# Layer 0 of a two-layer encoder: earlier gate modulation, conformer taps at other places, the short conv's taps beside the output projection

## The chip, the cores and the metric

The kernel runs as one program on one core of a Trainium2 chip. The metric is the device time of one execution in microseconds (us), lower is better. A core has a matrix engine (TensorE, PE), a vector engine (VectorE, DVE), a scalar engine (ScalarE, ACT), GpSimd (POOL), and SyncE (SP), whose queue issues the DMA transfers here. Each engine takes its instructions in the order of its own queue; an instruction that waits holds up all that stand behind it on that queue.

## The reference

For each of two layers, on x of 256 positions by 2048 channels, with a condition vector c:

```python
mod = (silu(c) @ w_mod[l] + b_mod[l]).reshape(bn, 6, d)
shift_m, scale_m, gate_m, shift_f, scale_f, gate_f = ...
h = layer_norm(x) * (1.0 + scale_m) + shift_m
uv, q_c, kv_c, k_r, sb, sc, sh, ag = split(h @ w_in[l])
y_a = gmlp_mixer(uv, ...)                 # u * (W_s LN(v) + b), 128-position blocks
y_b = mla_mixer(q_c, kv_c, k_r, ...)      # attention from latents, rotary key
y_c = sb * causal_dwconv(sc * sh, w_conv) # short conv, 3 taps
y_d = conformer_conv(ag, ...)             # GLU, 31 taps, LayerNorm, swish
y = concatenate([y_a, y_b, y_c, y_d]) @ w_out[l]
x = layer_norm(ALPHA * x + (1.0 + gate_m) * y, ...)
h = layer_norm(x) * (1.0 + scale_f) + shift_f
x = layer_norm(ALPHA * x + (1.0 + gate_f) * conv_ffn(h, ...), ...)
```

Everything is float32. Many products are made of three products of split numbers (a high part "hi" and a remainder "lo", both in the faster fp32r form): lo is made on DVE by a subtraction (L462, tile wlo), hi on ACT by a cast (L461, tile whi).

## The kernel before, in words

**Stages of layer 0.** The shared normalised input is made in five pieces over the contraction; within each, products of the conformer's (D), gMLP's (U, V) and short conv's gate (E) columns are accumulated (`by_pieces`, PIECES). Then come, in the order of TensorE's work:

- the latents, stage **B** (`latent_group`, eight units of two contraction tiles, tiles B_w and B_n, exact fp32 products). Beside them DVE does the gMLP's norm (`mix_v`, tile va, L1004 to L1032) and TensorE its mixing products (ps_mix). At its end `mix_b` squares and copies the latents on ACT (L1062 to L1075);
- the short conv's columns, stage **C** (`group`, eight units, tile C_c). The attention (`attend`, which starts with the transposes ps_q at L1087) is "postponed": its instructions come behind the first unit of C. At the end `mix_c` multiplies into chC, `conv_c` makes three taps over four channel blocks (one ACT scaling and two DVE multiply-adds a block, L1250 to L1261, tile yc), and `mix_e` multiplies by the gate E (L1264);
- the **output projection** (`out_proj`, tile o). Its first chunk of 1024 columns has eight units of two contraction tiles, and the order of the contraction is a, b, c, d: yc is read from its ninth tile on. Two more chunks of 512 columns follow with exact products ("plain": 1024 and 1536).

**What runs beside them.** `stream` is called once for each unit: it issues the unit's weight load, then the products of the unit before, then pumps the modulation, then takes some blocks from a list called `background`:

```python
item = load()
flush()
pending.append(lambda: products(item))
if mods:
    pump()
for _ in range(min(bg, len(background))):
    background.pop(0)()
```

The **modulation stream** (`mod_stream`) loads w_mod in rows of 128x2048 (1024 KB, tile wmod, SP's queue) and adds each into an accumulator with one DVE multiply-add (L240, tile macc; the first of a sum is L238). Sixteen loads make one vector; GATE_M comes first in layer 0, then SHIFT_F and SCALE_F; all 48 are needed by the end of the output projection. For a gate, a bias row is loaded behind the sixteenth (L354, tile brow) and added on DVE (L358); then `gate_rows` lets TensorE sum it over the partitions (ps_gate, four quarters, as "chores" of later pumps). For a shift or scale the sum is ps_mod. `pump` adds the stage's rate in RATES to a credit and takes one step for each whole credit. The loads' buffers are four "raw" tiles; split weights and bias rows use the same four, so a modulation load on SP's queue waits until DVE has used the load four back, and weights queued behind it on SP wait as well.

The **background** of layer 0 is the conformer's 31 taps and its norm (`conv_d` with `taps`: four ACT scalings to the tile scaled, L919, in two buffers, then one DVE addition to convD, L920; norm_d at the end). STEPS says how many are taken per unit: one in B, three in C. What is left at the end of C is drained there.

The queue of each engine is laid out when the program is built, by a scheduler that follows these calls and its own costs; a product can thus stand ahead of, or behind, others that the source names in another order.

Of the kernel before, what the change touches and what calls it, by code (L numbers as in the profile page):

```python
# [18 lines left out]
KT = D // P  # L19
# [13 lines left out]


RATES = [
    dict(B=1.6, C=2.2, out=1.5, up=0.7, down=0.7),
    dict(D=1.0, U=0.0, V=0.0, B=0.0, C=0.0, E=0.9, out=0.6, up=0.3, down=0.7),
]

STEPS = [  # L40
    dict(B=1, C=3, up=2),
    dict(U=7, B=4, C=4, E=8, up=2),
]

PIECES = ((0, 2), (2, 2), (4, 4), (8, 4), (12, 4))
# [5 lines left out]
def encoder_kernel(ctx: ExitStack, tc: tile.TileContext, A: dict, consts: bass.AP, out: bass.AP):  # L51
# [321 lines left out]
    def phase(l, name):  # L373
        pace["rate"] = RATES[l][name]
# [26 lines left out]
    def drain_background():  # L401
        while background:
            background.pop(0)()
# [214 lines left out]
    def run(g):  # L618
        units, load, products, end, bg = g
        for u in range(units):  # L620
            stream(lambda: load(u), lambda item, u=u: products(item, u), bg)
            pending.extend(postponed)
            postponed.clear()
        pending.append(end)
# [44 lines left out]
    def out_proj(l, w, src, order, gate_of, name, post_g, post_b, before, then, plain=(), bg=0):  # L669
# [113 lines left out]
        for c0, width in CHUNKS:  # L783
            last = c0 + width == D
            nk = 2048 // width
            units = nkt // nk
            state = {"tail": []}

            def load(u, c0=c0, width=width, nk=nk, units=units, last=last):
                item = load_unit(u, c0, width, nk, units, last)  # L790
                if last and u == units - 1:
                    gains()
                return item

            def load_unit(u, c0, width, nk, units, last):
                kt = order[nk * u]
                assert order[nk * u : nk * u + nk] == list(range(kt, kt + nk))
                spare = nk if last and units - 4 <= u < units - 2 else 0
                exact = c0 in plain
                parts = weights(w, kt, nk, c0, width, exact, spare)  # L800
                s4 = src[kt // 4]
                if exact:
                    return parts, [(s4[:, kt % 4 + k, :], None) for k in range(nk)]
                acts = []
                for k in range(0, nk, 2):
                    pair = kept.get(kt + k)
                    if pair is None:
                        pair = act_pair("a")
                        split(pair, s4[:, kt % 4 + k : kt % 4 + k + 2, :])
                        if nkt == KT:  # L810
                            kept[kt + k] = pair
                    for j in range(2):
                        acts.append([h[:, j, :] for h in pair[:2]])
                return parts, acts

            def unit(item, u, state=state, c0=c0, width=width, nk=nk, last=last, units=units):
                if u == 0:
                    state["ps"] = [
                        [acc_tile(f"{name}_{c0}{t}{i}") for i in range(width // 512)] for t in range(2)
                    ]  # L820
                if last and u >= units - 4:
                    state["tail"].append((item, u))
                    return
                for t in range(2):
                    products(t, item, state["ps"], u, nk)

            for u in range(units):
                stream(lambda: load(u), lambda item, u=u, unit=unit: unit(item, u), bg, not last)

            def done(state=state, c0=c0, nk=nk, last=last):  # L830
                if c0 == 0:
                    box["gate"] = gate_of()
                for t in range(2):
                    for item, u in state["tail"]:
                        products(t, item, state["ps"], u, nk)
                    if t == 0 and last and before is not None:
                        before()
                for t in range(2):
                    finish(t, state["ps"], c0)
                    if last:  # L840
                        norm(t)
                if last:
                    closed.append(True)

            pending.append(done)


    def mixers(l, w_in, Y, hF=None, between=None):
# [397 lines left out]

        def conv_c(ch):
            yc = Y["c"] = slot("yc").rearrange("p (j s) -> p j s", j=4)
            for j in range(4):
                act.activation(out=yc[:, j, :], in_=ch[:, j, :], func=AF.Copy, scale=SW(2, j))  # L1250
                for k in range(2):
                    dve.scalar_tensor_tensor(
                        out=yc[:, j, 2 - k :],
                        in0=ch[:, j, : S - 2 + k],
                        scalar=SW(k, j),
                        in1=yc[:, j, 2 - k :],
                        op0=ALU.mult,
                        op1=ALU.add,
                    )

        def mix_e(cps, _):  # L1261
            yc = Y["c"]
# [36 lines left out]
    def by_pieces(l, w_in, hF, between, mix_d, mix_u, gelu_v, mix_v, mix_b, mix_c, mix_e):  # L1299
# [49 lines left out]
        for q, (k0, nkt) in enumerate(PIECES):  # L1349
            ahead = between(q + 1) if q + 1 < len(PIECES) else ([], None)  # L1350
            exact = k0 < PLAIN_KT
            loaded = {}

            def load(g, kt):

                c0, width = (C_AG, 1024) if g == "D" else (cols[g], 512)
                nk = min(2048 // width, nkt)
                for j, p in enumerate(weights(w_in, kt, nk, c0, width, exact or g != "D")):
                    loaded[(g, kt + j)] = p

            mods_left = list(ahead[0])
            units = len(mods_left)

            def some_mods(share):
                while mods_left and (units - len(mods_left)) < units * share:
                    mods_left.pop(0)()

            def d_part(kt, half):
                if ("D", kt) not in loaded:
                    load("D", kt)  # L1370
                chan_major(accD, kt, loaded[("D", kt)], range(4 * half, 4 * half + 4), kt == 0, kt == KT - 1)

            turns_d = [(kt, h) for kt in range(k0, k0 + nkt) for h in range(2)]
            n = len(turns_d) // 4
            for s in range(4):
                mine = turns_d[s * n : (s + 1) * n]
                if ("D", mine[0][0]) not in loaded:
                    load("D", mine[0][0])
                some_mods((0.3, 0.7, 1.0, 1.0)[s])
                if s == 3 and ahead[1] is not None:  # L1380
                    ahead[1]()
                for kt, h in mine:
                    d_part(kt, h)
                if s < 3:
                    g = "UVE"[s]
                    load(g, k0)
                    some_mods((0.5, 0.85, 1.0)[s])
                    side(g, [(kt, loaded[(g, kt)]) for kt in range(k0, k0 + nkt)], k0, nkt)
        mix_d(accD, None)
        mix_u(sums["U"], None)  # L1390
        for t in range(2):
# [5 lines left out]

        def mix_ce(cps, tps):
            mix_c(cps, tps)
            mix_e(sums["E"], None)  # L1400

        run(group(w_in, C_SC, 1024, f"C{l}", mix_ce, hF=hf, bg=STEPS[l]["C"]))
        drain_background()
# [151 lines left out]
    for l in range(DEPTH):  # L1555
        Y = {}
        if l == 0:
            hF = [slot(f"hF{q}").rearrange("p (j s) -> p j s", j=4) for q in range(4)]
            mixers(l, A["w_in"][l], Y, hF, lambda q: piece(q, hF))
        else:  # L1560
            mixers(l, A["w_in"][l], Y)
        phase(l, "out")
        flush()
        out_proj(
            l,
            A["w_out"][l],
            [Y[n] for n in "abcd"],
            list(range(KT)),
            gate(l, GATE_M),
            f"o{l}",  # L1570
            A["post_mix_g"][l],
            A["post_mix_b"][l],
            needs(l, SHIFT_F, SCALE_F),
            modulated(l, SHIFT_F, SCALE_F),
            plain=(1024, 1536) if l == 0 else (),
        )
        phase(l, "up")
        if l + 1 < DEPTH:
            turns.extend(load_params(l + 1))
        G = []  # L1580
        ffn_up(l, G)
        phase(l, "down")
        flush()
        out_proj(
            l,
            A["ffn_w_down"][l],
            G,
            list(range(NF)),
            gate(l, GATE_F),
            f"d{l}",  # L1590
            A["post_ffn_g"][l],
            A["post_ffn_b"][l],
            needs(l + 1, SHIFT_M, SCALE_M) if l + 1 < DEPTH else None,
            modulated(l + 1, SHIFT_M, SCALE_M) if l + 1 < DEPTH else None,
        )
# [63 lines left out]
```

## Time and profile before

| | us |
|---|---|
| median of 3 runs (2279.96 to 2282.76) | 2281.75 |
| the profiled execution | 2284.06 |
| its span in the trace | 2282.3 |
| TensorE busy | 2216.6 (97%) |
| VectorE busy | 1781.2 (78%) |
| ScalarE busy | 1111.3 (49%) |
| stage B of layer 0 | 189.92 to 233.89 |
| stage C with attention | 233.89 to 330.46 |
| first chunk of the output projection | 330.46 to 388.47 |
| the other two chunks | 388.47 to 448.75 |

A profile is one execution; the time outside the span is 1.76 us. Rows of its views read so: a timeline row is start, duration, engine, line of the kernel, operation, tile written <- tiles read, shapes, and how many records the row joins; in brackets is the engine's idle time in front of it and what ended that. A group row is the same without a start: count, then total busy time, mean of one in ns, then the idle time ahead of these instructions. "PEclk" is the TensorE clock that was granted, as a share of full speed. An fp32 matmul leaves two records.

### The profile page before, as it was taken

To read this page: it belongs to the slowest core of one execution; us is meant where nothing else is said; L and a number is where in the kernel's file an instruction comes from. 1 tells how busy PE (TensorE), PEld (TensorE's weight loads), DVE (VectorE), ACT (ScalarE), POOL (GpSimd) and SP (SyncE) were. 2 spreads that over 40 slices of the span, in tenths; PEclk is the share of its full clock that TensorE was granted. 3 is DMA by queue.
4 is the path that set the end of the run, shared out by engine and by line. 5 is a ranking of instruction groups with operands and counts; after the bars stand their busy time and mean duration, and the time that the engine had idled before them with its cause. 6 is when DMAs were issued, how large, how long until landed. Compare 5 with 4: busy or idle time off the path is not lost. (4 is left out here: it accounts for less than half of the span.)

```text
span 2282.3 us, 28994 instructions
## 1 busy us (share of the span) xinstructions
PE 2216.6 (97%) x11118; PEld 1823.0 (80%) x11118; DVE 1781.2 (78%) x2192; ACT 1111.3 (49%) x1693; POOL 37.2 (2%) x61
## 2 busy tenths in 40 slices
PE   5899999999999999999999999999999999999997
PEld 4686777478888888887886888877888888888886
DVE  6877889588899899898977997887776565565676
ACT  2234652264554554544556545556555454454553
POOL 2000000000000000000000000000000000000000
PEclk9999999999999999999999999999999999999999
DMA  9999879778888988888875755966665555555554
GB/s 348 368 336 337 334 261 379 282 263 327 309 326 300 333 312 327 318 318 295 323 269 195 236 186 175 328 247 226 240 224 183 195 182 194 190 196 187 197 190 147
DMA packets 228691, 604.11 MB, mean 265 GB/s; under 512 B 14580, under 2 KB 27108, under 8 KB 206788
## 3 DMA queue, kind: packets, MB, share of 16 engines
q1 hardware_dynamic: 227704, 601.25, 74.3%
q8 instruction: 87, 1.43, 0.2%
q0 software_dynamic: 848, 1.01, 0.1%
q14 instruction: 52, 0.43, 0.0%
HBM read 600.11 MB, written 2.10 MB: 264 GB/s over the span
## 5 line engine op out<-in xcount | busy, mean ns | idle before, releaser
L461 ACT CAST whi<-wraw 128x1024 fp32r<-128x1024 f32 (+1 forms) x624 | 649.7, 1048 | 705.6 <-PE g_c L79 198.6
L462 DVE TENSOR_TENSOR wlo<-wraw,whi 128x1024 fp32r<-128x1024 f32 (+1 forms) x624 | 749.0, 1214 | 309.0 <-ACT whi L461 301.8
L79 PE MATMUL v_c<-hT,whi 128*128 128x512 f32 x1408 | 491.4, 393 | 0.0
L79 PE MATMUL g_c<-hT,whi 128*128 128x512 f32 x1280 | 446.8, 393 | 0.0
L79 PE MATMUL v_c<-hT,wlo 128*128 128x256 f32 x1408 | 394.1, 280 | 0.0
L79 PE MATMUL d<-whi,a 128*128 128x512 f32 x1344 | 387.9, 390 | 0.0
L240 DVE SCALAR_TENSOR_TENSOR macc<-wmod,cact,macc 128x2048 f32<-128x2048 f32 x150 | 352.0, 2347 | 18.2 <-DMA wmod<-in_w_mod_dram 18.0
L79 PE MATMUL g_c<-hT,wlo 128*128 128x256 f32 x1280 | 358.2, 280 | 0.0
L79 PEld LDWEIGHTS v_c<-hT,whi 128*128 128x128 f32 x1408 | 263.6, 187 | 59.5
L79 PEld LDWEIGHTS d<-whi,a 128*128 128x128 f32 x1344 | 252.8, 188 | 52.6
L79 PEld LDWEIGHTS g_c<-hT,whi 128*128 128x128 f32 x1280 | 239.7, 187 | 54.3
L79 PEld LDWEIGHTS v_c<-hT,wlo 128*128 128x128 f32 x1408 | 265.8, 189 | 0.2
L79 PEld LDWEIGHTS g_c<-hT,wlo 128*128 128x128 f32 x1280 | 241.7, 189 | 0.2
L79 PE MATMUL d<-wlo,a 128*128 128x512 f32 x672 | 233.7, 390 | 1.9 <-DVE wlo L462 1.9
L79 PEld LDWEIGHTS d<-wlo,a 128*128 128x128 f32 x672 | 126.5, 188 | 29.0 <-DVE wlo L462 2.7
L79 PE MATMUL o<-whi,a 128*128 128x512 f32 x352 | 102.4, 398 | 0.0
L480 ACT CAST a<-g 128x512 fp32r<-128x512 f32 x132 | 81.3, 617 | 36.0 <-PE d L79 33.3
L481 DVE TENSOR_TENSOR a<-g,a 128x512 fp32r<-128x512 f32 x132 | 87.8, 685 | 1.8 <-ACT a L480 1.8
L605 PE MATMUL first<-wexact,hN 128*128 128x512 f32 x192 | 85.5, 595 | 1.2 <-ACT hN L82 0.8
L240 DVE SCALAR_TENSOR_TENSOR qacc<-wmod,cact,qacc 128x1024 f32<-128x1024 f32 (+1 forms) x75 | 80.2, 1070 | 2.4 <-DMA wmod<-in_w_mod_dram 0.4
L79 PEld LDWEIGHTS o<-whi,a 128*128 128x128 f32 x352 | 67.1, 192 | 15.3 <-ACT whi L461 1.0
L1448 DVE SCALAR_TENSOR_TENSOR u<-g,pf,u 128x254 f32<-128x254 f32 (+1 forms) x176 | 73.8, 479 | 0.4 <-ACT u L82 0.2
(355 smaller groups left out, 2497.6 us busy)
## 6 DMA issues: line engine op xcount, KB each, us to landing
wraw<-in_ffn_w_up_dram SPq DMA_DIRECT2D x168, 1024.0 KB, 5.2
wmod<-in_w_mod_dram SPq DMA_DIRECT2D x160, 1024.0 KB, 6.5
wraw<-in_ffn_w_down_dram SPq DMA_DIRECT2D x88, 1024.0 KB, 5.2
wmod<-in_w_mod_dram SPq DMA_DIRECT2D x64, 512.0 KB, 7.4
wraw<-in_w_in_dram SPq DMA_DIRECT2D x30, 1024.0 KB, 7.2
wexact<-in_w_in_dram SPq DMA_DIRECT2D x52, 512.0 KB, 7.6
wraw<-in_w_out_dram SPq DMA_DIRECT2D x24, 1024.0 KB, 6.5
wexact<-in_w_out_dram SPq DMA_DIRECT2D x16, 512.0 KB, 12.7
```

Source lines behind the costliest of these rows:

```text
L79: pe.matmul(o, lhsT, rhs, start=start, stop=stop, skip_group_check=True)
L240: i = dve.scalar_tensor_tensor(out=acc, in0=w, scalar=col, in1=acc, op0=ALU.mult, op1=ALU.add)
L461: held(act.copy(hi[:, :m], r), "cast")
L462: i = dve.tensor_tensor(out=lo[:, :m], in0=r, in1=hi[:, :m].bitcast(F32), op=ALU.subtract)
L480: act.copy(hi, src)
L481: dve.tensor_tensor(out=lo, in0=src, in1=hi.bitcast(F32), op=ALU.subtract)
L605: i = pe.matmul(ps, hN[kt // 4][:, kt % 4, t * P : (t + 1) * P], parts[kt], start=kt == 0, stop=kt == KT - 1, skip_group_check=True,)
L1448: dve.scalar_tensor_tensor(out=u[:, sh:], in0=x[:, : S - sh], scalar=col(k, j), in1=u[:, sh:], op0=ALU.mult, op1=ALU.add)
```

## The change

It touches layer 0 alone, in four places that belong together.

- Rates of the modulation: the last piece now pumps too (three times at a rate of 2.0, so six steps of GATE_M), B goes from 1.6 to 1.5 a unit, C from 2.2 to 2.4, the output projection from 1.5 to 0.95. The sum over the layer's stages stays about the same (48.4 before, 48.6 after).
- Conformer taps: two in each unit of B instead of one; in C none in the first two units, three in each of the other six.
- The short conv's taps: `conv_c` no longer emits its four blocks at once but puts them into the background, and `mix_e` behind them as a fifth. The output projection takes two a unit, and at the ninth contraction tile of its first chunk (where yc is first read) drains what is left.
- `run` takes a list of counts, one a unit, beside a number.

```diff
 RATES = [
-    dict(B=1.6, C=2.2, out=1.5, up=0.7, down=0.7),
+    dict(last=2.0, B=1.5, C=2.4, out=0.95, up=0.7, down=0.7),
...
 STEPS = [
-    dict(B=1, C=3, up=2),
-    dict(U=7, B=4, C=4, E=8, up=2),
+    dict(B=2, C=(0, 0, 3, 3, 3, 3, 3, 3), out=2, up=2),
+    dict(U=7, B=4, C=4, E=8, out=0, up=2),
 ]
...
     def run(g):
         units, load, products, end, bg = g
         for u in range(units):
-            stream(lambda: load(u), lambda item, u=u: products(item, u), bg)
+            steps = bg if isinstance(bg, int) else bg[u]
+            stream(lambda: load(u), lambda item, u=u: products(item, u), steps)
...
             def load_unit(u, c0, width, nk, units, last):
                 kt = order[nk * u]
+                if nkt == KT and c0 == 0 and kt == KT // 2:
+                    drain_background()
...
         def conv_c(ch):
             yc = Y["c"] = slot("yc").rearrange("p (j s) -> p j s", j=4)
-            for j in range(4):
+
+            def block(j):
                 act.activation(out=yc[:, j, :], in_=ch[:, j, :], func=AF.Copy, scale=SW(2, j))
                 for k in range(2):
                     dve.scalar_tensor_tensor(
...
+            for j in range(4):
+                if hF is None:
+                    block(j)
+                else:
+                    background.append(lambda j=j: block(j))
...
             n = len(turns_d) // 4
+            if q == len(PIECES) - 1:
+                phase(l, "last")
             for s in range(4):
...
                     side(g, [(kt, loaded[(g, kt)]) for kt in range(k0, k0 + nkt)], k0, nkt)
+                    if q == len(PIECES) - 1:
+                        pump()
...
         def mix_ce(cps, tps):
             mix_c(cps, tps)
-            mix_e(sums["E"], None)
+            background.append(lambda: mix_e(sums["E"], None))
...
             plain=(1024, 1536) if l == 0 else (),
+            bg=STEPS[l]["out"],
         )
```

In the changed program's queues, as built, these things stand elsewhere: on TensorE's queue the first ps_gate and the first ps_q come right behind B's last product and ahead of C's first, where before both came in C; on DVE's queue the bias row of GATE_M comes behind the twelfth conformer tap of B, with the taps that follow it ahead of the latents' key products (kc); ps_mod of SHIFT_F comes just ahead of the output projection instead of in its first chunk.

## The prediction

> **What bounds the kernel now.** The page first: the span and the busy time of each engine.
>
> ```profile
> span 2282.3 us, 28994 instructions
> PE 2216.6 (97%) x11118; PEld 1823.0 (80%) x11118; DVE 1781.2 (78%) x2192; ACT 1111.3 (49%) x1693; POOL 37.2 (2%) x61
> ```
>
> TensorE (PE) is busy for 2216.6 of 2282.3 us. The change neither adds nor removes a matmul, so it can move only the 66 us in which PE idles and the time in which its clock is reduced. So the next view is the table by stretches; its columns are the stretch and its length, the busy time (and instructions) of PE, PEld, DVE, ACT, POOL, then the granted clock, the DMA share and GB/s. I cut layer 0 into latents (B), short-conv group with attention (C) and first chunk of the output projection, and three windows of 10 us inside them.
>
> ```profile
> 189.92:233.89 43.97, 41.78 (x146) 27.52 (x145) 38.47 (x39) 26.11 (x61) 1.64 (x2) 0.96 0.94 339
> 233.89:330.46 96.57, 94.03 (x432) 77.46 (x430) 77.88 (x85) 54.80 (x133) 2.33 (x4) 0.96 0.80 306
> 330.46:388.47 58.01, 52.78 (x226) 41.30 (x225) 53.17 (x51) 19.86 (x26) 0.00 (x0) 0.94 0.90 334
> ...
> 200.00:210.00 10.00, 7.82 (x31) 5.89 (x31) 9.03 (x19) 3.33 (x8) 1.64 (x2) 0.83 0.74 289
> ...
> 240.00:250.00 10.00, 7.67 (x26) 4.86 (x25) 9.50 (x10) 7.06 (x18) 0.00 (x0) 0.71 0.60 219
> 340.00:350.00 10.00, 7.34 (x25) 5.89 (x26) 10.00 (x11) 4.25 (x6) 0.00 (x0) 0.83 0.97 340
> ```
>
> PE idles 2.19 us in B, 2.54 in C and 5.23 in the first chunk, with a clock under 0.9 only around those idles. That is all the change can win in these stages; what it can lose has no such lid. PE's waits between 185 and 460 us say what ended the idles (columns: total, times, longest).
>
> ```profile
> PE o L79 <- DVE wlo L462: 4.9, 2, 4.7
> PE ps_mix L79 <- DVE va L1013: 2.2, 1, 2.2
> PE ps_q L1087 <- ACT qg L1093: 1.6, 1, 1.6
> ```
>
> The first two are VectorE (DVE) work in front of what PE needs, and they are what the change can reach.
>
> **Part 1, the gMLP wait in B.** Timeline of DVE and of PE.
>
> ```profile
> 190.79 1.28 DVE L864 TENSOR_TENSOR gluD<-D_c,sg 128x512 f32<-128x512 f32 x2
> 195.31 2.35 DVE L240 SCALAR_TENSOR_TENSOR macc<-wmod,cact,macc 128x2048 f32<-128x2048 f32 x1 [3.24 <-DMA wmod<-in_w_mod_dram]
> ```
>
> ```profile
> 189.49 0.60 PE L1002 MATMUL ps_wT<-cst,gmlp 128*128 128x128 f32 x4
> 189.92 0.81 PE L79 MATMUL B_w<-wexact,hF 128*128 128x384 f32 x2
> ...
> 199.39 0.81 PE L79 MATMUL B_w<-wexact,hF 128*128 128x384 f32 x2
> 202.38 3.43 PE L79 MATMUL ps_mix<-wT,va 128*128 128x128 f32 x16 [2.19 <-DVE va L1013]
> ```
>
> DVE waited 3.24 us for a modulation load ahead of the gMLP norm, so va came at 202.9 and PE stood 2.19 us. From 189.92 to 199.39 lie eight rounds of four matmuls, 1.184 us each; B's 128 matmuls are 32 rounds, 37.9 us. ps_mix at the pace of ps_wT (0.43 for 4) is 1.7 instead of 3.43. So B's floor is 39.6 us, and it loses 4.3: 2.19 idle and 2.1 of reduced clock behind it. In the changed program six loads of GATE_M are issued in the last piece, so that multiply-add no longer waits: va is ready between 198.4 (if gluD needs no macc ahead of it) and 199.6 (195.31 becomes 192.0), and PE comes to ps_mix at about 198.9. I take **−4.3 us**: B's last product at 229.5 instead of 233.89.
>
> The clock's share of it stands in the stretch right behind that wait:
>
> ```profile
> 202.38:206.00 3.62, 3.62 (x17) 3.42 (x18) 2.65 (x5) 1.70 (x4) 0.00 (x0) 0.62 1.04 425
> ```
>
> It was 0.62 there, after an idle of 2.19 us. The Trainium skill ("TensorE: Matmul & The Clock Gate", Part 1: The HAM clock gate) states that the clock falls to half after an idle window of about 3.4 us. By that rule alone 2.19 us would not have to cost any clock, part 1 would be worth 2.2, and the sum below would be +4.8. The row decides against it.
>
> **Part 2, what this puts at the end of B.** The costs of one DVE step, from the groups of B:
>
> ```profile
> L240 DVE SCALAR_TENSOR_TENSOR macc<-wmod,cact,macc 128x2048 f32<-128x2048 f32 x8 | 18.8, 2347 | 4.3 <-DMA wmod<-in_w_mod_dram 4.3
> L920 DVE TENSOR_TENSOR convD<-convD,scaled 128x1020 f32<-128x1020 f32 (+10 forms) x11 | 13.1, 1195 | 0.6 <-ACT scaled L919 0.5
> ```
>
> In the timeline neighbours overlap a little: from start to start a multiply-add takes 2.27, a tap 1.11. The bias row and, later in C, four records of gate products:
>
> ```profile
> 260.70 2.27 DVE L358 TENSOR_TENSOR macc<-macc,brow 1x2048 f32<-1x2048 f32 x1
> ```
>
> ```profile
> 309.32 1.96 PE L79 MATMUL ps_gate<-macc,ones 128*128 128x512 f32 x4
> ```
>
> Before, the bias row came at 260.7 and the gate products in the midst of C, waited for by nobody. In the changed program the first ps_gate (two such records, 0.9) and the first ps_q stand on PE's queue **ahead of every product of C**, right behind B. ps_gate waits for the bias row, and on DVE ahead of that row stand, from va's end on, 12 taps, 9 multiply-adds and the rest of the gMLP: 12 × 1.11 + 9 × 2.27 + 2.8 = 36.5 us, then the row itself, 2.2. From 198.4 that is 237.1; PE has been done since 229.5. So PE waits some 7.5 us for DVE.
>
> Then ps_q, which waits for ScalarE's (ACT's) third latent tile. ACT at this place, before:
>
> ```profile
> 230.32 2.06 ACT L919 ACTIVATE scaled<-gluD,pm 128x245 f32<-128x245 f32 x5 [1.68 <-DVE convD L920]
> 232.37 0.48 ACT L1062 ACTIVATE junk<-B_w 128x384 f32<-128x384 f32 x1
> ...
> 235.69 0.39 ACT L1069 COPY lat<-B_w 128x256 f32<-128x256 f32 x1
> ```
>
> Two sets of scaled taps (four ACT calls of 0.42, 1.7 us a set) now stand ahead of the latents on ACT, and each needs the buffer that a tap behind the bias row on DVE frees: 237.1 + 1.1 + 1.7 + 1.7 = 241.6. From the first square (232.37) to the third tile's copy it took 3.3 us, of which 0.4 was a scaled tap: about 2.7. So ps_q can run at 244.3, and C's first product at about **244.5 instead of 233.89, +10.6** (−4.3 of part 1 is in it). Bounds: below, if ACT's two sets overlap the wait for the bias row, C starts at 240.7, +6.8; above, with va at 199.6 and each set waiting a whole tap more, 248, +14. I take 10.6, nearest to the summed rows.
>
> What hides in the gap comes off in C: ps_gate, −0.9. C of before loses 2.54 idle and some 2.8 of clock (0.71 in 240:250), 5.3 in all, most of it at these rows:
>
> ```profile
> 240.80 0.60 PE L1087 MATMUL ps_q<-cst,lat 128*128 128x128 f32 x4
> 244.88 2.04 PE L79 MATMUL ps_kr<-kc,cst 64*128 64x256 f32 x4 [0.20 <-DVE kc L1100]
> ```
>
> The same chain from latents to queries follows in the changed program, on a clock that has gone down once. Eight taps and two multiply-adds stand between the bias row and kc: 237.1 + 8 × 1.11 + 2 × 2.27 = 250.5, or 252 at ACT's 1.7 a set; both are about the end of C's first 32 products. I count 4.8, −0.5. DVE's load in C (77.88 of 96.57) falls, with 16 taps left instead of 24. SP's queue: C's first weights go out behind a modulation load freed near 228, its second behind one that needs the bias row's buffer (237). One 512-KB load of this kind was on its way 12.5 us in the stretch 207:233:
>
> ```profile
> wexact<-in_w_in_dram SPq DMA_DIRECT2D x4, 512.0 KB, 12.5
> ```
>
> So they land at about 241 and 249.5, ahead of 244.5 and of the end of C's first 32 products, about 252. Cost 0, with 2.5 us to spare; if that cover fails, see the second rival. Lag at the end of C: 10.6 − 0.9 − 0.5 = **+9.2**.
>
> **Part 3, the output projection.** Timeline of PE and of DVE in the first chunk.
>
> ```profile
> 342.65 0.79 PE L79 MATMUL o<-wlo,a 128*128 128x512 f32 x2 [4.74 <-DVE wlo L462]
> ...
> 347.11 1.08 PE L79 MATMUL o<-whi,a 128*128 128x512 f32 x4
> ...
> 353.93 1.73 PE L79 MATMUL o<-whi,a 128*128 128x512 f32 x6
> 355.50 3.63 PE L79 MATMUL ps_mod<-ones,macc 128*128 128x1 f32 x32
> 358.98 0.70 PE L79 MATMUL o<-wlo,a 128*128 128x512 f32 x2
> ```
>
> ```profile
> 334.76 2.35 DVE L240 SCALAR_TENSOR_TENSOR macc<-wmod,cact,macc 128x2048 f32<-128x2048 f32 x1
> 337.02 3.24 DVE L1252 SCALAR_TENSOR_TENSOR yc<-chC,pm,yc 128x254 f32<-128x254 f32 x8
> 340.17 1.29 DVE L1264 TENSOR_TENSOR yc<-yc,sumE 128x512 f32<-128x512 f32 x2
> 341.38 2.36 DVE L462 TENSOR_TENSOR wlo<-wraw,whi 128x1024 fp32r<-128x1024 f32 x2
> ```
>
> From 347.11 to 353.93 thirty matmuls take 6.82, 0.2273 each; 192 of them are 43.6, with ps_mod (3.5) 47.1 of 58.01. The chunk **loses 10.9**: 4.74 is the short conv's 3.24 and its gating's 1.29 ahead of a weight remainder, the rest clock (0.83 in 340:350) and small waits. The change spreads these over the first three units and pumps 0.95 loads a unit instead of 1.5. Per unit of 24 matmuls (5.45 us of PE) DVE then has two remainders (2.26), 0.95 × 2.27 = 2.16 and four short-conv taps (3.24/8 × 4 = 1.6): 6.0, half a microsecond too much in units one to three, so waits of 0.7, 0.6 and 0.4 remain; later units have 4.4 of DVE for 5.45 of PE. With 1.2 of clock behind those waits and 1.5 at the start (ps_mod, moved just ahead of the chunk, leaves the clock low as it does from 358.98 on) the loss is 4.4: **−6.5**. Bounds: 0 (the stall only changes its name) and −10.9.
>
> What comes after (other chunks, feed-forward, layer 1) has the same steps; its modulation steps shift by one pump at most: 0, ±2.
>
> **The sum**: +9.2 − 6.5 = **+2.7 us**. The profiled execution took 2284.06 (span 2282.3 and 1.76 around it); with the change 2286.8. The median of the runs is 2281.75, and the forecast from there is **2284.5 us**.
>
> **The rivals.**
> 1. *Both stages come down to their floors.* The early gate rows leave C without its 5.3 and the chunk without its 10.9: 10.6 − 0.9 − 5.3 − 10.9 = −6.5, **2275.3**. For it: DVE has fewer multiply-adds in the chunk (7.6 instead of 12). Against it: the latents' chain remains.
> 2. *Slower: C's second weights come late.* Their issue on SP hangs on the buffer that the bias row frees. If they land later than 252, PE stops; with the 12.5 counted from 243.5 (two loads of 1024 KB that stand ahead, served first) they come at 256 to 258, +6, **2290.5**. It decides from a bias row later than about 239.5 on.
> 3. *The change does nothing at the projection*: the remainder waits for a multiply-add where it waited for the short conv; half of the 10.9 stays lost beyond my 4.4: +4.5, **2289**.
> 4. *The clock restarts once more.* Part 1 priced a restart at 2.1. The two waits at B's end are divided by one ps_gate; if each brings a restart, or the one comes later and falls on C's dense products, that is +2.1, **2286.6**. For it: PE works under 1 us between them, and the 1.6 on qg follows. Against it: the first restart would pass while PE idles anyway.
>
> **How the numbers follow.** A measurement of this kernel can tell about 0.2% (4.6 us) from no change, so the bounds are 2277.2 and 2286.3. Forecast 0.42, of which 0.29 lie within and 0.13 above (the start of C at up to +14); rival 1, 0.16, faster; rival 2, 0.17 and rival 3, 0.12, slower; rival 4, 0.13, of which 0.05 within. Faster 0.16, same 0.34, slower 0.50. The range goes from rival 1 to rival 2, 2275 to 2291; the forecast's own is 2281 to 2288.
>
> **What would show it.** Right: no wait of ps_mix on va; a wait of ps_gate on DVE's bias row of 6 to 8 us and of ps_q on ACT of about 6 right behind it; C's first product near 244.5; a first chunk of 48 us (without ps_mod) with no wait over 1 us. Wrong: C starting before 238 (parts 1 and 2 then win), a wait on a weight load in C's second unit (rival 2), a wait of 3 us or more on wlo (rival 3).

## The result and the profile after

The changed kernel takes 2285.69 us (median of 13 runs, 2282.15 to 2290.07), the kernel before, beside it, 2280.93 (13 runs, 2276.28 to 2283.79). The ratio is 1.002 with a 95% interval of 1.0013 to 1.0028: some 4.8 us slower. The forecast was +2.7. The profile below is of the first of the 13 executions, which took 2290.07, the longest of them; its stages can be longer than those of a typical one.

The page of the profile after says that nothing was saved or added in work:

```profile
span 2288.2 us, 29020 instructions
...
PE 2216.8 (97%) x11118; PEld 1823.4 (80%) x11118; DVE 1781.0 (78%) x2192; ACT 1109.1 (48%) x1693; POOL 36.2 (2%) x61
```

TensorE's busy time is the same as before within 0.2 us, so the difference is idle time and clock. The table by stretches of the changed kernel, with the same columns as before: B up to C's first product, C, and the first chunk of the projection (with ps_mod ahead of it).

```profile
193.08:248.14 55.06, 42.67 (x149) 26.52 (x148) 54.09 (x49) 34.98 (x87) 1.64 (x2) 0.93 0.92 340
248.14:342.49 94.35, 92.96 (x428) 77.75 (x428) 72.76 (x82) 43.99 (x106) 2.33 (x4) 0.97 0.78 305
342.49:393.77 51.28, 50.53 (x226) 41.60 (x225) 47.34 (x47) 21.25 (x28) 0.00 (x0) 0.93 0.85 302
```

The first stretch was 43.97 and is 55.06; DVE is busy in 54.09 of it, PE in 42.67. The chunk was 58.01 and is 51.28. So the change does at the projection what it says, and pays at the end of B. PE's waits from 185 to 470 us name the payment:

```profile
PE ps_gate L79 <- DVE macc L358: 5.7, 1, 5.7
PE ps_q L1090 <- ACT lat L1072: 4.8, 1, 4.8
PE B_w L79 <- DMA wexact<-in_w_in_dram: 1.9, 2, 1.5
PE o L79 <- ACT whi L461: 0.7, 1, 0.7
```

The waits on va and on wlo of before are gone; two new ones stand in a row. The timelines of PE, DVE and ACT show how they hang together:

```profile
240.98 2.05 PE L79 MATMUL ps_gate<-macc,ones 128*128 128x512 f32 x2 [5.67 <-DVE macc L358]
247.87 0.48 PE L1090 MATMUL ps_q<-cst,lat 128*128 128x128 f32 x1 [4.84 <-ACT lat L1072]
248.14 8.47 PE L79 MATMUL C_c<-hF,wexact 128*128 128x256 f32 x32
...
259.07 1.10 PE L79 MATMUL ps_kr<-kc,cst 64*128 64x256 f32 x4 [0.21 <-DVE kc L1103]
```

```profile
238.56 2.27 DVE L358 TENSOR_TENSOR macc<-macc,brow 1x2048 f32<-1x2048 f32 x1
240.76 2.42 DVE L923 TENSOR_TENSOR convD<-convD,scaled 128x972 f32<-128x972 f32 x2
```

```profile
241.95 3.20 ACT L922 ACTIVATE scaled<-gluD,pm 128x241 f32<-128x241 f32 x8 [1.61 <-DVE convD L923]
245.06 0.47 ACT L1065 ACTIVATE junk<-B_w 128x384 f32<-128x384 f32 x1
...
247.46 0.36 ACT L1072 COPY lat<-B_w 128x256 f32<-128x256 f32 x1
```

Read from the bottom: the latents' copy came at 247.46 since ACT did two sets of scaled taps from 241.95 on, and these had waited for the tap that stands behind the bias row on DVE (240.76), and the row had come at 238.56. C's first 32 products then took 8.47 instead of 7.07, on a clock that had gone down: it was granted at 0.50 from 241.00 to 248.14, at 0.63 up to 252.00 and at 1.00 up to 256.50.

One thing in this profile isn't the change's. B starts at 193.08, 3.16 us later than in the profile before, though the DMA issues ahead of the last piece are the same in both programs; the unchanged kernel, profiled a second time (below), starts B at 192.96. So stages are compared from B's start on.

### The profile page after: what moved, and what is told of

The parts are those of the page before. It is cut to its first block, busy times and chain, and to the rows that moved or that the text cites. A ratio compares the mean times of both kernels' runs of the same rounds, so it can differ in the third digit from the quotient of the medians.

```text
span 2288.2 us, 29020 instructions
## 1 busy us (share of the span) xinstructions
PE 2216.8 (97%) x11118; PEld 1823.4 (80%) x11118; DVE 1781.0 (78%) x2192; ACT 1109.1 (48%) x1693; POOL 36.2 (2%) x61
## 5 line engine op out<-in xcount | busy, mean ns | idle before, releaser
L79 PEld LDWEIGHTS v_c<-hT,whi 128*128 128x128 f32 x1408 | 263.8, 187 | 60.6
```

The costliest lines, as they stand in the source:

```text
L79: pe.matmul(o, lhsT, rhs, start=start, stop=stop, skip_group_check=True)
```

## The experiments

The theory: the gate's first product and the first transpose, ahead of C's products, wait for a bias row and for latents that come late; what the projection wins is less. The rivals: the queue positions alone; the sum of DVE's work in B and C; the loads. All stage times in the table are starts read from one profile of each kernel, counted from B's first product: C is C's first product, ps_kr are the key products at the head of the attention, ps_sc its scores; the last column is the end of the projection's first chunk.

| kernel | median us | before beside it | ratio (95%) | C | ps_kr | ps_sc | chunk's end |
|---|---|---|---|---|---|---|---|
| before, first profile | 2281.75 | | | 43.97 | 54.96 | 79.90 | 198.55 |
| before again | 2283.14 (one time) | 2281.47 | | 39.81 | 51.12 | 76.22 | 193.53 |
| changed | 2285.69 | 2280.93 | 1.002 (1.0013 to 1.0028) | 55.06 | 65.99 | 90.42 | 200.69 |
| short conv alone | 2280.23 | 2281.15 | 0.9998 (0.9988 to 1.0009) | 40.63 | 51.95 | 76.64 | 193.32 |
| short conv and rate | 2287.84 | 2281.15 | 1.0033 (1.002 to 1.0045) | 40.80 | 52.12 | 76.95 | 201.87 |
| taps back | 2288.74 | 2281.15 | 1.0034 (1.0023 to 1.0046) | 50.27 | 66.49 | 92.75 | 203.33 |
| gate in C | 2290.87 | 2281.15 | 1.0042 (1.0027 to 1.0057) | 39.66 | 53.86 | 78.51 | 200.97 |
| gate late | 2285.19 | 2281.47 | 1.0022 (1.0012 to 1.0032) | 55.56 | 67.55 | 89.63 | 201.59 |
| both late | 2288.94 | 2281.47 | 1.0041 (1.0029 to 1.0053) | 45.94 | 66.22 | 91.98 | 203.97 |
| both late, latents first | 2278.57 | 2281.47 | 0.9986 (0.9978 to 0.9995) | 44.00 | 56.29 | 79.82 | 193.24 |
| latents first alone | 2272.60 | 2281.89 | 0.9966 (0.9953 to 0.9978) | 44.50 | 54.22 | 75.65 | 186.82 |
| before, latents first | 2282.25 | 2281.89 | 1.0004 (0.9994 to 1.0013) | 40.42 | 58.79 | 81.68 | 193.29 |
| conv at once | 2281.51 | 2281.89 | 0.9998 (0.9988 to 1.0008) | 44.84 | 56.07 | 80.06 | 197.41 |
| other rates | 2281.70 | 2281.89 | 1.0003 (0.9994 to 1.0013) | 39.65 | 53.18 | 78.99 | 195.90 |

### The kernel before, a second profile

No edit.

> The kernel before, unchanged, in a second profile. In the traces with the same instructions in B (short conv alone; short conv and rate) B took 40.6 and 40.8 us and va kept the matrix engine waiting 0.5 and 0.7, where the first profile of the kernel before had 44.0 and 2.2. Theory (the 3.24-us wait for a modulation load, and with it the 4.3 that B lost, belongs to that one execution): B 40 to 41.5 us, wait on va under 1. Rival (the kernel before always loses it): B 43.5 to 44.5, wait on va 2 or more.

The theory held. B took 39.81, its floor of the prediction (39.6), and the wait on va is gone. The stretch of B first, then DVE's row:

```profile
192.96:232.77 39.81, 39.81 (x147) 26.16 (x146) 37.79 (x39) 25.43 (x60) 1.64 (x2) 1.00 1.01 369
```

```profile
195.83 2.35 DVE L240 SCALAR_TENSOR_TENSOR macc<-wmod,cact,macc 128x2048 f32<-128x2048 f32 x1 [1.30 <-DMA wmod<-in_w_mod_dram]
```

The load that DVE had waited 3.24 us for in the first profile cost 1.30 here, PE's idle time went to 0. The projection's stall, on the other hand, came again, to within a hundredth (4.75; its row stands in the last section). So the first was a matter of one execution; the second is in both.

### Short conv alone

The kernel before with `conv_c` and `mix_e` in the background and two of them a unit beside the projection; all rates and taps as before.

```diff
-    dict(last=2.0, B=1.5, C=2.4, out=0.95, up=0.7, down=0.7),
+    dict(last=0.0, B=1.6, C=2.2, out=1.5, up=0.7, down=0.7),
-    dict(B=2, C=(0, 0, 3, 3, 3, 3, 3, 3), out=2, up=2),
+    dict(B=1, C=3, out=2, up=2),
```

> Only the short conv's taps and its gating go beside the output projection; rates and conformer taps as before. Theory (the chunk gains because its vector work per unit falls below the matrix engine's 5.45 us, which needs the lower pump rate as well): with 1.5 loads a unit the vector engine has 3.4 + 2.26 + 1.6 = 7.3 us in the first units, so most of the stall is only cut into pieces; chunk 55 to 58 us instead of 58.0, time 0 to 3 us below before. Rival (the lump of 4.5 us in front of one weight remainder is all that matters): chunk 51 to 52 us, time 5 to 7 us below before.

Chunk 56.04 (58.01 and 56.68 in the two profiles before), no measurable change in time. The stall was cut into pieces, as the theory said: four waits on wlo, 4.5 us together. The two longest, from PE's timeline:

```profile
338.20 0.73 PE L79 MATMUL o<-wlo,a 128*128 128x512 f32 x2 [1.96 <-DVE wlo L462]
360.45 0.74 PE L79 MATMUL o<-wlo,a 128*128 128x512 f32 x2 [1.86 <-DVE wlo L462]
```

### Short conv and rate

As above, with `C=3.0, out=0.95`.

> Short conv beside the projection and 0.95 loads a unit there; the loads that this saves go into stage C (3.0 a unit), nothing is pumped in the last piece, conformer taps as before. Theory (the end of B is where the change loses, the projection where it gains): B and the start of C as before (44 us after B's start), chunk with ps_mod 51 to 52 us; stage C has 6.4 multiply-adds more, 14.5 us of vector work on 77.9 of 96.6, and may lose 0 to 2; time 5 to 7 us below before. Rival (early gate and early taps are what keeps C free for this): C longer by 4 to 7 us, time within 2 us of before.

The rival's mechanism held, and by more than it said: C up to ps_mod took 107.1 us (147.89 less 40.80) instead of 97, and the time is 6.7 above before, where the rival had "within 2". Part of it is two waits for the softmax on DVE, which has more multiply-adds to do in C at 3.0 loads a unit than at 2.2. PE's timeline:

```profile
291.19 0.63 PE L1205 MATMUL ps_pT<-cst,p 128*128 128x128 f32 x4 [2.82 <-DVE p L1196]
303.18 0.57 PE L1205 MATMUL ps_pT<-cst,p 128*128 128x128 f32 x2 [3.16 <-DVE p L1196]
```

So C doesn't take the loads that the projection gives up without a loss. Nor was the projection cured: with both the short conv's blocks spread and 0.95 loads a unit, one wait of 3.27 on wlo was left in its first chunk (53.98 with ps_mod, where 51 to 52 were expected).

### Taps back

The changed kernel with one tap a unit in B.

```diff
-    dict(B=2, C=(0, 0, 3, 3, 3, 3, 3, 3), out=2, up=2),
+    dict(B=1, C=3, out=2, up=2),
```

> The changed kernel with one conformer tap a unit in B and three in C, as before; early gate rows kept. Theory (the bias row comes late because 12 taps and 9 multiply-adds stand ahead of it): eight taps less are 8.9 us, the row is there 39 us after B's start, before the matrix engine's last product of B (42); no wait of ps_gate over 1 us, C's first product 42 to 44 us after B's start instead of 55; time 7 to 10 us below the changed kernel, 2276 to 2279. Rival (the loads hurried into the last piece and B are the cause, whatever the taps): ps_gate still waits 4 us or more, time within 3 us of the changed kernel.

A miss: 3 us above the changed kernel, though the two intervals overlap, with a wait of ps_gate of 7.73. DVE's timeline says why: of the tap additions ahead of the bias row none had gone. The last of them and the row:

```profile
235.33 1.17 DVE L923 TENSOR_TENSOR convD<-convD,scaled 128x976 f32<-128x976 f32 x1
236.41 2.27 DVE L358 TENSOR_TENSOR macc<-macc,brow 1x2048 f32<-1x2048 f32 x1
```

The tap of 976 columns is the twelfth, as in the changed kernel. The scheduler had put the taps that the source names in C into B. STEPS asks; it does not place. So this run tests neither the theory nor its rival: the taps ahead of the bias row were as many as before.

### Gate in C

The changed kernel with `B=1.2, C=2.7`.

> The changed kernel with B at 1.2 loads a unit and C at 2.7, so that the bias row and the first ps_gate come in C behind its first products; the two taps a unit in B stay. Theory (it is the place of ps_gate and ps_q ahead of C's products that costs): C's first product 42 to 45 us after B's start instead of 55, the latents' chain hidden behind C's first unit; time 6 to 10 us below the changed kernel, 2276 to 2280. Rival (the doubled taps hold ScalarE and with it the latents): ps_q still waits 4 us or more behind C's first unit, time 2281 to 2285.

C starts at 39.66, 15.4 us earlier than in the changed kernel, and the time is 2290.87, the highest of all. C itself takes 106.93. The first half of the theory (what holds C's start) stands; the second (that C's start is what counts) fell. The rival fell too: ps_q waited 0.6. C's idle time is spread: 3.0 us of ps_qr waiting for DVE, 2.4 of C's own products waiting for the latents' copy, 1.5 at the conformer's norm; how much of it comes from the loads and how much from the late latents this run doesn't show. Its table by stretches:

```profile
192.29:231.95 39.66, 39.66 (x147) 26.11 (x146) 39.35 (x39) 25.57 (x58) 1.64 (x2) 1.00 0.94 348
231.95:338.88 106.93, 97.58 (x431) 79.24 (x430) 85.78 (x93) 54.77 (x137) 2.32 (x4) 0.95 0.80 307
```

### Gate late

The changed kernel; the first gate's sums wait for the sixth load of SHIFT_F.

```diff
-                if 1 <= kt < KT - 1:
+                if (6 if (l, m) == (0, SHIFT_F) else 1) <= kt < KT - 1:
```

> The changed kernel, but the gate's sums over the partitions wait for the sixth load of SHIFT_F, so that ps_gate goes far into C; loads, taps and the bias row stay where they are, and ps_q still stands ahead of C's products. Theory (two holds in a row: behind ps_gate's wait stands ps_q's, whose latents come late since ScalarE's taps wait for the taps behind the bias row): no wait of ps_gate, but one wait of ps_q of 9 to 12 us; C's first product still 53 to 55 us after B's start, time within 2 us of the changed kernel. Rival (ps_gate alone holds the matrix engine): C's first product at 43 to 47, time 5 to 10 us below the changed kernel.

The theory held, with a wait a little above its 9 to 12: ps_gate's wait went, and ps_q's took its place whole.

```profile
246.98 0.96 PE L1090 MATMUL ps_q<-cst,lat 128*128 128x128 f32 x2 [12.65 <-ACT lat L1072]
247.74 9.56 PE L79 MATMUL C_c<-hF,wexact 128*128 128x256 f32 x32
```

### Both late

As above, and ps_q ordered behind the latest product.

```diff
-                    pe.transpose(ps[0:n, o + t * P : o + (t + 1) * P], parts[t], ident)
+                    i = pe.transpose(ps[0:n, o + t * P : o + (t + 1) * P], parts[t], ident)
+                    if behind is not None:
+                        tc.add_manual_dep(i.ins, behind, order_dep, reason="the first unit's products come first")
```

> As the one with the late gate, and the attention's first transposes (ps_q) are held behind the products of C's first unit on the matrix engine's queue, as before the change. Theory (the queue positions are the loss): C's first product 41 to 43 us after B's start, ps_q's wait 4 to 7 us behind the 7 us of C's first products; time 4 to 8 us below the changed kernel, 2278 to 2282. Rival (the vector engine has too much to do in B and C together, so what is won at C's start is lost inside C, as in the kernel with 1.2 and 2.7): C longer by as much, time within 2 us of the changed kernel.

My theory fell here. C's first product came at 45.94 instead of 55.06, and the key products still at 66.22 (65.99 in the changed kernel). PE ran half of C's first products early and then waited for the latents all the same:

```profile
245.77 5.41 PE L81 MATMUL C_c<-hF,wexact 128*128 128x256 f32 x16 [4.51 <-ACT lat L1072]
251.01 0.60 PE L1094 MATMUL ps_q<-cst,lat 128*128 128x128 f32 x4
255.84 0.99 PE L1094 MATMUL ps_q<-cst,lat 128*128 128x128 f32 x4 [4.23 <-ACT qg L1102]
```

What is late is the latents, not the products. The wait in the middle of C's first products ends on the latents' copy too: the kernel has six accumulators for these products (`accp`), and four hold the latents until ACT has copied them. C's first 16 records write two accumulators and the next 16 two more, so this fits; no run changes the number of accumulators. In the table the kernels with the changed kernel's rates fall into two groups by ps_kr (66 to 68 us, or 54 to 56) and by time; the column of C's start does not sort them. That is the new theory, of which this run is no test yet: ACT's scalings of taps ahead of the latents, with the DVE taps and the bias row that they hang on, are the loss; the queue position of ps_gate and ps_q is not.

### Both late, latents first

As above, with one tap a unit in B and three in C, and on ACT every scaling that is named after `mix_b` ordered behind the latents:

```diff
+                latents[0] = i.ins.name if hF is not None else None
...
+                    if latents[0] is not None:
+                        tc.add_manual_dep(i.ins, latents[0], order_dep, reason="the latents come first")
```

> As the one before (late gate, ps_q behind C's first products), with one conformer tap a unit in B and three in C, and ScalarE's scalings of the taps that follow held behind the latents. Theory of the queue positions: latents ready 45 us after B's start, no wait of ps_q over 2 us, key products some 3 to 5 us earlier than with both late alone; time 7 to 12 us below the changed kernel, 2274 to 2279. Rival (vector work in B and C): 24 taps instead of 16 are left for C, which loses at the softmax or at the conformer's norm what its start won; time 2282 to 2287.

2278.57, below both kernels and, as expected, 7 below the changed one; ps_kr at 56.29, ten us earlier than with both late. C's first product still waits, now for its weights:

```profile
235.45 8.68 PE L82 MATMUL C_c<-hF,wexact 128*128 128x256 f32 x32 [2.46 <-DMA wexact<-in_w_in_dram]
```

### Latents first alone

The last edit without the other two: ps_gate and ps_q stand ahead of C's products again, as in the changed kernel. Against "taps back" it differs by the order on ACT alone.

> The kernel that won, without the late gate and without the hold on ps_q: of its three edits only the conformer's taps (one a unit in B, three in C, and behind the latents on ScalarE) are left on the changed kernel. ps_gate and ps_q stand ahead of C's products again. Theory (the taps ahead of the bias row and of the latents make the hold long, the queue positions only make it visible): bias row four taps earlier, about 43 us after B's start, latents at 45, C's first product at 45 to 48 instead of 55; time 1 to 4 us above the kernel that won and 3 to 7 below the changed kernel. Rival (the queue positions alone): C's first product at 52 to 55, time within 2 of the changed kernel.

The fastest of all: 2272.60, a ratio of 0.9966 (0.9953 to 0.9978), 13 us below the changed kernel and 16 below "taps back". It is also 6 below "both late, latents first", where I had expected 1 to 4 above. In both, C's first product comes 44 us after B's start, with its weights. Here ps_gate and ps_q run ahead of that, PE's longest wait is 1.34 and C's first 32 products take 7.17; there PE stood 2.46 in one piece, and they took 8.68. So the early ps_gate and ps_q are not the loss, and here they fill a wait. The order on ACT also changed DVE's queue: seven tap additions stand ahead of the bias row instead of twelve; ACT has finished its taps when B ends, and DVE has the row soon after:

```profile
232.21 0.47 ACT L1071 ACTIVATE junk<-B_w 128x384 f32<-128x384 f32 x1 [9.16 <-PE B_w L82]
```

```profile
225.66 7.12 DVE L244 SCALAR_TENSOR_TENSOR macc<-wmod,cact,macc 128x2048 f32<-128x2048 f32 x3
232.81 2.28 DVE L362 TENSOR_TENSOR macc<-macc,brow 1x2048 f32<-1x2048 f32 x1
```

```profile
235.24 1.10 PE L82 MATMUL ps_gate<-macc,ones 128*128 128x512 f32 x2 [1.34 <-DVE macc L362]
236.17 0.38 PE L1098 MATMUL ps_q<-cst,lat 128*128 128x128 f32 x2
237.13 7.17 PE L82 MATMUL C_c<-hF,wexact 128*128 128x256 f32 x32 [0.58 <-DMA wexact<-in_w_in_dram]
```

The waits at C's start are 1.34 and 0.58, ps_q has none, and the clock does not go down. The stretches, to be read against those of the changed kernel:

```profile
192.63:237.13 44.50, 41.40 (x150) 26.38 (x149) 44.05 (x40) 21.89 (x55) 2.57 (x3) 1.00 0.91 354
237.13:327.81 90.68, 89.78 (x426) 75.31 (x427) 81.66 (x90) 56.64 (x137) 1.40 (x4) 1.00 0.92 350
327.81:379.45 51.64, 50.52 (x226) 41.60 (x225) 47.70 (x48) 21.83 (x28) 0.00 (x0) 0.93 0.85 300
```

B is 10.6 shorter, C 3.7, at a granted clock of 1.00 in both; the chunk is the same (51.64 to 51.28).

### The kernel before with the latents first

> The kernel before with one edit: the scalings of the taps that follow stand behind the latents on ScalarE. Theory (before the change the latents' chain hid behind C's first products but for 1.6 to 1.9 us): time 0 to 2 us below before. Rival (that edit alone is what made the winning kernel faster): time 3 us or more below before, same as the winner.

No measurable gain, as the theory had it: by time it is not an improvement by itself, but the repair of what the change did. Inside, a loss and a gain cancel. Its ps_kr came later, 58.79; DVE's multiply-adds stood ahead of kc there, with ps_kv waiting 4.63 us for DVE. And its first chunk took 51.43 (193.29 less 141.86) instead of 56.68, with no wait over 0.9, though the short conv and the rates are those of before: the first four weight remainders now stand ahead of the short conv's 3.24 us on DVE's queue.

### Conv at once

"Both late, latents first", with the short conv's four blocks and the gating emitted at once, as before the change.

> The kernel that won, with the short conv's taps and gating back where they were before the change (at once, behind C's products). Theory (at 0.95 loads a unit the lump of 4.5 us still stands ahead of a weight remainder, but the vector engine has slack to catch up): one wait of 2 to 4 us in the chunk, time 1 to 4 us above the winner. Rival (the pump rate is the whole gain there): within 1 us of the winner.

Ratio 0.9998 against 0.9986; the intervals overlap, so the 3 us are not clear by time. The chunk with ps_mod is 56.98 instead of 53.05. The stall is back, though the rate is 0.95:

```profile
343.50 1.22 PE L82 MATMUL o<-wlo,a 128*128 128x512 f32 x2 [3.65 <-DVE wlo L466]
```

So in these kernels neither half does it alone: the short conv alone won nothing that can be measured, and the rate alone leaves 3.65. That both are needed, or are enough, is not shown: "short conv and rate" and "gate in C" have both and wait 3.27 and 3.42 on wlo, "before, latents first" has neither and waits 0.53. What stands ahead of the first remainders on DVE's queue decides, and the two edits are one way to change it.

### Other rates

"Both late, latents first" with `B=1.3, out=1.1`.

> The kernel that won, with B at 1.3 loads a unit instead of 1.5 and the projection at 1.1 instead of 0.95. Theory (C's first weights come 2.5 us late and B's 1.2 since modulation loads stand ahead of them on SP's queue, and two of those are gone): the waits on weights fall under 1.5 us together; the projection has 2.7 us more vector work in a chunk with room; time 0 to 3 us below the winner. Rival (the chunk's first units have no room): a wait on a remainder of 3 us or more there, time 0 to 3 above the winner.

The rival held in its wait and its time: the weight waits in B and C went (C starts at 39.65), and the projection got a wait of 3.05 on a remainder, though in the middle of the chunk and not in its first units; the time is 3 us above the kernel it was made from, with intervals that just touch. And C's earlier start won nothing: ps_q waited 3.92 for ACT (1.42 in that kernel), and ps_mod comes 140.18 us after B's start as against 140.19.

## Why the prediction was right, and where not

**Direction and size.** Forecast +2.7, measured +4.8 (ratio 1.0013 to 1.0028), inside the range. The two profiles differ by 5.9 us in their spans: 3.16 at B's start, which is not the change's, +2.1 from there to the end of the chunk (200.69 less 198.55), 0.6 behind it. That the forecast came so near is luck in part, as part 1 shows.

**Part 1 was wrong.** "I take −4.3 us": the 2.19-us wait and its clock came from one execution. The second profile of the same kernel lost 0.2 of the 4.3, the three kernels with the same loads in B 1.0, 1.2 and 0.8 (40.63, 40.80 and 40.42 against the floor of 39.6). There was next to nothing to win, and the step that failed is to price a wait for a DMA from a single profile. And the changed kernel's B ended 42.2 after its start (240.98 less the wait of 5.67, less 193.08), with 1.9 us of waits on weights behind modulation loads on SP's queue, which I had at zero. Against the second profile before, the change costs 7.2 up to the chunk's end (200.69 less 193.53); the measured 4.8 lies between the two. Worked out from the second profile, the prediction's own rows put C's first product 14.8 late and not 10.6 (54.6 less 39.81), and its sum would have been +6.9.

**Part 2 was right by its rows.** Bias row done 47.2 us after B's start (237.1 less 189.92) forecast, 47.7 measured (240.76 less 193.08); C's first product 54.6 forecast, 55.06 measured; wait of ps_gate 7.5 forecast, 5.67 measured, since B ended later; ps_q about 6 forecast, 4.84 measured. From the first square to the third tile's copy 2.7 were put in, where the row's 3.3 less 0.4 is 2.9; it took 2.40. The keys kc, forecast for 60.6 to 62 us after B's start, came at 65.9, but PE waited only 0.21 for them. The lag at the end of C was forecast as +9.2 and is +8.9 against the first profile (149.41 less 140.54), +12.6 against the second. What it did not see is which link counts: I priced the place of two products on PE's queue, and "gate late" and "both late" show that the same lag stays when they are moved. The link is ACT's taps ahead of the latents: moved by an order on ACT alone ("taps back" against "latents first alone"), the lag turns into a gain. As that order also took five additions from ahead of the bias row, the two are not priced apart; that the latents' side suffices is seen where nothing waits for ps_gate ("both late" against the same with the latents first, ps_kr ten us earlier), though there the count of taps changed as well.

**Part 3 was right in size**: −6.5 forecast, −6.7 measured (51.28 less 58.01), −5.4 against the second profile. One wait of 0.71 is left where three of 0.4 to 0.7 were forecast. Neither edit gives it alone ("short conv alone", "conv at once"); the sum of DVE's work in a unit, from which it was forecast, is not the whole mechanism, since the order of DVE's queue alone gave a chunk of 51.43 ("before, latents first").

**The rest** (0, ±2 forecast): from the chunk's end to the end of the span 1894.4 against 1893.8, +0.6.

**The rivals.** Rival 1, both stages at their floor, did not happen in the changed kernel; "latents first alone" comes near it, with C at 90.68 (its floor is 90.4) and 2272.60 where 2275.3 was worked out, but its chunk of 51.64 is not at the floor of 47.1. Rival 2: no wait on weights in C of the changed kernel. Rival 3: no wait on wlo. Rival 4: one drop of the clock, as in the forecast: it stayed at 0.50 through the second wait, and C's first 32 products took 1.4 us more than at full clock.

## What to carry to other kernels

A stall in one profile is a term of the sum only if a second execution shows it: here a wait for a DMA was that run's (3.24 us, then 1.30), and a wait for work queued ahead on an engine came again (4.74, then 4.75). Moving filler work earlier is not free even where its engine idles: look which instruction of the critical chain then stands behind it, on every engine that the filler uses, here ACT's scalings as well as DVE's additions. A count of background steps does not place them where a scheduler decides the order; an ordering between two instructions does. The one here was worth 16 us between two kernels that differ by it alone, and nothing on the kernel before: what an order is worth depends on what else stands in the queues.

## What the runs showed of the hardware

The two profiles of the kernel before had the same wait of PE in the chunk, 4.74 and 4.75 us, but not the same slow products behind it. The first one's are in the prediction (0.79 for the pair at 342.65). The second's, from PE's timeline:

```profile
342.01 1.22 PE L79 MATMUL o<-wlo,a 128*128 128x512 f32 x2 [4.75 <-DVE wlo L462]
343.03 1.91 PE L79 MATMUL o<-whi,a 128*128 128x512 f32 x4
```

Here the first pair was already slow (1.22). In the first profile the clock was still granted in full during the wait (1.00 from 338.00 to 342.60) and fell behind it (0.61 from 342.65 to 347.00); in the second it had fallen within the wait (0.72 from 337.26 to 342.00, then 0.50 up to 346.00). The Trainium skill ("TensorE: Matmul & The Clock Gate", Part 1: The HAM clock gate) says that the activity window is free-running, so that the point of change depends on where in it the work falls; these two profiles agree with that. The idle window of some 3.4 us that the Trainium skill gives in the same section doesn't fit the clock of 0.62 behind a wait of 2.19 in the first profile.
